# Seven pairs of attention column blocks of the input projection, in part as seven products of 2x2 blocks

## The chip, the cores and the metric

The kernel runs on one core of one Trainium2 chip. The metric is the device time of one execution in microseconds. The median of three runs of the kernel before is 1010.01 us (1008.98 to 1010.36).

## The reference, cut to what matters

One layer of a hybrid decoder trunk, all in float32: 16 learned meta tokens stand ahead of 512 tokens (528 in all), and the width is 2048. After an RMS norm one input projection feeds three mixers side by side: gated DeltaNet (6 heads of 128), GLA linear attention (5 heads, 64 by 128) and forgetting attention (5 heads of 128). Each mixer's output is multiplied by the SiLU of its own gate columns; the three are joined, go through one output projection, and are added to the input; a final RMS norm follows.

```
proj = (rms_norm(x) @ w_in)                       # 528 x 2048 @ 2048 x 7585
(dq, dk, dv, dz, db, da, gq, gk, gv, gz, gl, fq, fk, fv, fz, ff) = split_cols(proj)
o_dn  = gated_delta_rule(silu(conv(dq, dk, dv)), ...)  -> head norm -> * silu(dz)
o_gla = gla(gq, gk, gv, gates of gl)                   -> head norm -> * silu(gz)
o_fox = softmax(fq.fk / sqrt(d) + c_t - c_s, causal) @ fv           -> * silu(fz)
out   = rms_norm(x + concat(o_dn, o_gla, o_fox) @ w_out)[:, 16:]
```

For the change, the columns `fk`, `fv`, `fq` and `fz` of the attention heads matter: each is a block of 128 columns per head, a 2048 x 128 matrix that multiplies the 528 (or, where meta tokens aren't needed, 512) columns of x transposed.

## The kernel before, in words

**Precision.** TensorE works on float32 values rounded to a shorter form (fp32r). So each operand is split exactly into a high and a low part, and each product is three matmuls: high by high, high by low, low by high. `split` makes the parts of a weight tile: a cast on ScalarE (L150) and a subtraction on VectorE (L151). x is kept on chip as 16 k-tiles of 128 rows in two parts, `xh[k]` and `xl[k]`, of 528 columns each.

**Input projection.** It goes block by block (128 columns). `inproj` loads the block's weights in two halves of 128 x 1024 (eight k-tiles, 512 KB, buffer `raw`), splits them (`whi`, `wlo`; two buffers of each kind, pool `wp`), and accumulates in PSUM tiles `pp` of the pool `psb` (four banks). A block that needs the meta tokens is two column ranges of 264, so 16 x 3 x 2 = 96 matmuls; one without them is a single range of 512, 48 matmuls (all at L207). `evac` (L325, L327) or `gate_z` multiplies the result by the row scale `rstd` on VectorE.

**Order.** The program is written group by group: DeltaNet heads 0 to 2 (keys, values, queries, a triangular inverse, then the recurrence over four blocks of tokens), DeltaNet heads 3 to 5, the GLA gates, three GLA pairs, and five attention heads (`fox_head`: keys, values, queries, gate; then per block of 128 queries scores, softmax and transposes, and at the end the sum over values). A scheduler orders every engine's instructions ahead of time by a simulated timeline; an engine then runs its queue strictly in that order. TensorE's order mixes one head's mixer with the projection of the blocks to come. `behind` and the tables `PLACE` and `PM` tie a few mixer matmuls behind a given number of projection matmuls. `paced` ties an instruction behind the last split so far.

**Output projection.** Eight of its sixteen input blocks (six DeltaNet, two GLA) are already computed as seven products of 2x2 blocks instead of eight. Sums of the weights for this are made by `weight_sums(j, half)` beside the attention: four loads of 256 KB, four subtractions on VectorE (L432), four stores to HBM tile `tw`. Before, heads 0 to 3 make two each (table `SUMS`). Sums of the left operands are made by `first_sums` (L459, L460) in head 4 on VectorE; the gated mixer outputs `zs` that they read stay on chip all the time, in the pool `zp` of eleven buffers. The matmuls of the output projection stand at L1068, the last VectorE and GpSimd steps at L1082 to L1092.

**Pools that the change touches:** `zp` (mixer gates), `six` (eight large buffers), `row` (seven buffers of one row of 531), `psb` (four PSUM banks of the projection).

Of the kernel before, what the change touches and what calls it, by code (L numbers as in the profile page):

```python
# [8 lines left out]
F32 = mybir.dt.float32  # L9
F32R = mybir.dt.float32r  # L10
# [21 lines left out]

DN_HEADS, GLA_HEADS, FOX_HEADS = 6, 5, 5
SH = 8
R0 = 32
R1 = R0 + 17

# [41 lines left out]
def tile_hybrid_trunk(ctx, tc, xT, xtok, mtok, w_gate, w_in, w_out, w_dn, consts, lmask, fin_w, out, dbg=None):  # L79
# [4 lines left out]
    cst = pool("cst", 1)  # L84
    hp = pool("hp", 2 * KT)
    wp = pool("wp", 2)
    zp = pool("zp", 11)
    six = pool("six", 8)
    wk = pool("wk", 2)
    psb = pool("psb", 4, space=PSUM)  # L90
# [3 lines left out]
    def row(name, dt=F32):  # L94
        return wk.tile([P, 3 + T], dt, tag="row", bufs=7, name=name)
# [246 lines left out]
    def gate_z(kind, h, t=None):  # L342
        parts = inproj((kind, h), meta=False)
        p_, t0, n = parts[0]
        z = row(f"z{kind}{h}")[:, :T]
        V.tensor_tensor(out=z[:, :S], in0=p_, in1=rstd[:, t0 : t0 + n], op=ALU.mult)
        if t is None:
            t = zp.tile([P, S], F32, tag="zs", name=f"zs{kind}{h}")
        silu(t, z[:, :S], f"{kind}{h}")
        zs[kind, h] = t  # L350

# [53 lines left out]
    dump("gcol", gcol[:, 0:4])  # L405


    def conv_silu(key, blk, dst, meta=True):
# [17 lines left out]
    def weight_sums(j, half):  # L426
# [16 lines left out]
        sub(x, x, z)  # L443
        put(3, x)

    heads = ([("dz", h) for h in range(DN_HEADS)] + [("gz", h) for h in range(GLA_HEADS)]
             + [("fz", h) for h in range(FOX_HEADS)])
    sub = lambda o, a, b: V.tensor_tensor(out=o, in0=a, in1=b, op=ALU.subtract)
    pairs = range(SH // 2)
    t0, t1 = slice(0, 256), slice(256, 512)  # L450
# [2 lines left out]
    def first_sums():  # L453

        s1 = six.tile([P, SH // 2, 256], F32, tag="six", name="s1")
        for j in pairs:
            a, b = (zs[heads[2 * j + i]] for i in range(2))
            raw[j] = r = dict(a11=a[:, t0], a12=b[:, t0], a21=a[:, t1], a22=b[:, t1], s1=s1[:, j], s3=a[:, t1])
            V.tensor_tensor(out=r["s1"], in0=r["a21"], in1=r["a22"], op=ALU.add)  # L459
# [283 lines left out]
    def gla_pair(p):  # L743
# [31 lines left out]
        a32 = wk.tile([P, 8, 32], F32, tag="a32", bufs=1, name=f"a32{p}")  # L775
        G.memset(a32, 0.0)
        at = ats[0]

# [114 lines left out]
        for e in range(ne):  # L893
# [11 lines left out]
                PE.transpose(pt[:, b * P : (b + 1) * P], on[:, b * P : (b + 1) * P], ident)  # L905
            o = zs["gz", 2 * p + e]
            V.scalar_tensor_tensor(out=o, in0=pt, scalar=glw[:, 0:1], in1=o, op0=ALU.mult, op1=ALU.mult)


    def fox_head(h):  # L910
        qk = six.tile([P, 3, T], F32, tag="six", name=f"fqk{h}")
        kT, qT = qk[:, 0], qk[:, 2]
        evac(inproj(("fk", h)), kT)

        v = row(f"vf{h}")[:, :T]
        evac(inproj(("fv", h)), v)
        pv = psm.tile([P, 512], F32, tag="m", name=f"pvf{h}")
        for b in range(NB):
            PE.transpose(pv[:, b * P : (b + 1) * P], v[:, bsl(b)], ident)
        vhi, vlo = (row(f"v{n}{h}", dt=F32R)[:, :S] for n in ("hi", "lo"))  # L920
        v3 = t15(f"v3{h}", (P, P))
        A.copy(vhi, pv)
        V.tensor_tensor(out=vlo, in0=pv, in1=vhi.bitcast(F32), op=ALU.subtract)
        A.copy(v3, pv[:, 3 * P :])
        v4 = t15(f"v4{h}", (P, 2 * NB, NM))
        G.tensor_copy(v4, v[:, 0:NM].unsqueeze(1).to_broadcast([P, 2 * NB, NM]))
        pw = psm.tile([P, 512], F32, tag="m", name=f"pwf{h}")
        PE.transpose(pw[:, :P], v4.rearrange("p b t -> p (b t)"), ident)
        vm = t15(f"fvm{h}", (P, 2, P), F32R)
        A.copy(vm[:, 0], pw[:, :P])  # L930
        V.tensor_tensor(out=vm[:, 1], in0=pw[:, :P], in1=vm[:, 0].bitcast(F32), op=ALU.subtract)
        evac(inproj(("fq", h), meta=False), qT, scale=float(P) ** -0.5)
        cc = six.tile([P, 2 * T + S], F32, tag="six", name=f"fc{h}")
        z = wk.tile([P, S], F32, tag="gd", name=f"fz{h}") if h < 2 else cc[:, T + S : T + 2 * S]
        gate_z("fz", h, z)
# [6 lines left out]
        if h == FS:  # L942
            first_sums()
        if h in SUMS:
            for j, half in SUMS[h]:
                weight_sums(j, half)
# [52 lines left out]
    PM = (308, 319)  # L999
    for g in range(2):  # L1000
# [15 lines left out]
    qts += [kq[0][:, 2 * S :], kq[1][:, :S]]  # L1016
    ats.append(kq[1][:, S:].rearrange("p (n t) -> p n t", t=P))
    for p in range(3):
        gla_pair(p)
    for h in range(GLA_HEADS):  # L1020
        dump(f"ogl{h}", zs["gz", h])
    for h in range(FOX_HEADS):
        fox_head(h)
    for h in range(FOX_HEADS):
        dump(f"ofx{h}", zs["fz", h])
# [4 lines left out]
            mybir.DependencyClass.NoSync, mybir.DependencyReason.DATA), reason="behind")  # L1030


    plain = heads[SH:]
    NP = len(plain)
    EARLY, LAST = NP - 2, NP - 6
# [17 lines left out]
    free = []  # L1053

    def begin(tb, cc, load=True):
        if len(acc) < 11 - SH:
            acc[tb, cc] = zp.tile([P, S], F32, tag="zs", name=f"acc{cc}{tb}")
# [173 lines left out]
def _layout(x, meta_tokens, norm_w, w_in, conv_w, a_log, dt_bias, dn_norm_w, w_gk2, b_gk,  # L1231
# [11 lines left out]
    wo = w_out[0][SH * P :].reshape((16 - SH) // 2, 2, P, 4, 512)  # L1243
# [44 lines left out]
```

## Time and profile before

| | |
|---|---|
| median of 3 runs | 1010.01 us |
| the profiled execution | 1010.53 us |
| its span, first to last instruction | 1008.8 us |
| TensorE matmul busy | 995.7 us, 7614 matmuls |
| VectorE, ScalarE, GpSimd busy | 618.2, 433.1, 138.6 us |
| bytes moved by DMA | 128.13 MB |

Busy time is the union of an engine's instructions. Matmuls overlap one another in it, so the mean duration of one is longer than the time that it adds; the distance between two starts is the better measure. In the groups, a row names the line, the engine, the operation, what it writes and reads, the shape and the count; then busy time and the mean of one in ns, and the idle time before them with what ended it. In timelines a row starts with its start and duration in us.

### The profile page before, as it was taken

How to read it: one execution, taken by the hardware profiler on the slowest of the kernel's cores; microseconds unless marked ns; L12 is line 12 of the kernel's file. 1: busy time of each engine (PE TensorE's matmuls, PEld its weight loads, DVE VectorE, ACT ScalarE, POOL GpSimd, SP SyncE). 2: the span in 40 equal slices, each digit the busy share in tenths (PEclk: the TensorE clock that was granted, in tenths of full speed). 3: DMA queues.
4: the chain of work that ended last, by engine and by line, in shares of the span. 5: the costliest groups of instructions: out<-in, count | busy, mean ns of one | idle time of the engine just before them, and what ended most of it. 6: DMA issues, size and time to landing. Idle time of an engine off the chain costs nothing.

```text
span 1008.8 us, 19003 instructions
## 1 busy us (share of the span) xinstructions
PE 995.7 (99%) x7614; PEld 898.7 (89%) x7614; DVE 618.2 (61%) x1342; ACT 433.1 (43%) x948; POOL 138.6 (14%) x141
## 2 busy tenths in 40 slices
PE   9999999999999999999999999999999999999996
PEld 7899999899999888898989988889898988888885
DVE  6366767865566985244646474655363747677673
ACT  7654533434456334244445444342323244354354
POOL 0021411211112322101111010100101010000060
PEclk9999999999999999999999999999999999999999
DMA  9623233233222223231221272543362635466634
GB/s 351 229 67 119 82 93 96 102 101 104 75 86 75 94 90 101 68 94 59 84 64 50 66 244 82 189 138 93 120 226 95 237 119 188 127 193 226 181 109 167
DMA packets 53357, 128.13 MB, mean 127 GB/s; under 512 B 11949, under 2 KB 15197, under 8 KB 53268
## 3 DMA queue, kind: packets, MB, share of 16 engines
q1 hardware_dynamic: 39008, 115.30, 34.5%
q10 hardware_dynamic: 14260, 11.61, 4.1%
q8 instruction: 60, 0.98, 0.4%
q14 instruction: 29, 0.24, 0.1%
HBM read 113.32 MB, written 13.44 MB: 126 GB/s over the span
## 4 chain that ended last, share of the span: by engine, by line
PE 92%; DVE 3%; ACT 1%; DMA 1%; POOL 1%; issue 1%; ACTq 1%; SPq 0%; DVEq 0%; POOLq 0%
PE pp L207 57%; PE pa L1068 5%; PE pq L1068 4%; PE pp L261 4%; PE pt L1068 4%; PE ps L1068 2%; PE pss L822 1%; PE pr L1068 1%; POOL stgz L334 1%; PE pgate L361 1%; PE pfo L990 1%; PE pfa L957 1%; DVE wlo L151 1%; DVE ot L556 1%; PE pg L523 1%
## 5 line engine op out<-in xcount | busy, mean ns | idle before, releaser
L207 PE MATMUL pp<-xl,whi 128*128 128x264 f32 (+2 forms) x1456 | 378.1, 310 | 0.0
L207 PE MATMUL pp<-xh,whi 128*128 128x264 f32 (+2 forms) x1456 | 376.3, 310 | 0.8 <-DVE fqk L325 0.7
L207 PE MATMUL pp<-xh,wlo 128*128 128x264 f32 (+2 forms) x1456 | 375.4, 309 | 0.4 <-DVE wlo L151 0.4
L207 PEld LDWEIGHTS pp<-xh,whi 128*128 128x128 f32 x1456 | 243.1, 188 | 15.1 <-issue 1.4
L207 PEld LDWEIGHTS pp<-xl,whi 128*128 128x128 f32 x1456 | 244.3, 189 | 13.6 <-issue 0.2
L207 PEld LDWEIGHTS pp<-xh,wlo 128*128 128x128 f32 x1456 | 243.7, 188 | 14.1 <-DVE wlo L151 0.8
L150 ACT CAST whi<-raw 128x1024 fp32r<-128x1024 f32 x110 | 115.3, 1048 | 184.7 <-PE pp L207 158.1
L151 DVE TENSOR_TENSOR wlo<-raw,whi 128x1024 fp32r<-128x1024 f32 x110 | 134.4, 1222 | 88.8 <-ACT whi L150 78.2
L334 POOL TENSOR_SCALAR stc<-cv 128x528 f32<-128x528 f32 (+1 forms) x18 | 28.2, 1566 | 138.2 <-DVE cv L418 115.2
L418 DVE SCALAR_TENSOR_TENSOR cv<-pb,cpk,cv 128x528 f32<-128x528 f32 (+1 forms) x54 | 40.7, 755 | 0.7
L1068 PE MATMUL pa<-whio,ol 128*128 128x512 f32 x72 | 28.5, 396 | 0.0
L1068 PE MATMUL pa<-wloo,oh 128*128 128x512 f32 x72 | 28.3, 393 | 0.0
L325 DVE TENSOR_TENSOR pb<-pp,rstd 128x264 f32<-128x264 f32 (+1 forms) x36 | 13.7, 423 | 23.3 <-PE pp L207 23.3
L432 DVE TENSOR_TENSOR ws<-ws 128x512 f32<-128x512 f32 x32 | 21.6, 686 | 9.7 <-DMA ws<-in_w_dn 9.6
L150 ACT CAST whis<-raws 128x1024 fp32r<-128x1024 f32 x16 | 16.8, 1051 | 24.8 <-PE pq L1068 9.7
L151 DVE TENSOR_TENSOR wlos<-raws,whis 128x1024 fp32r<-128x1024 f32 x16 | 19.5, 1222 | 12.7 <-ACT whis L150 12.7
L1068 PE MATMUL pa<-whio,oh 128*128 128x512 f32 x72 | 26.6, 399 | 0.0
L977 ACT CAST fphi<-pfx 128x384 fp32r<-128x384 f32 (+2 forms) x20 | 8.0, 399 | 41.0 <-PE pfx L974 38.2
L966 ACT ACTIVATE fp<-fp,fsm 128x144 f32<-128x144 f32 (+3 forms) x20 | 11.5, 574 | 29.8 <-DVE fsm L965 29.7
L150 ACT CAST whio<-rawo 128x1024 fp32r<-128x1024 f32 x13 | 13.7, 1051 | 24.1 <-PE pa L1068 12.8
L334 POOL TENSOR_SCALAR stfz<-zfz 128x512 f32<-128x512 f32 x5 | 10.6, 2126 | 94.9 <-ACT whi L150 47.8
L1092 POOL TENSOR_TENSOR acc<-acc,fw 128x512 f32<-128x512 f32 x3 | 4.6, 1564 | 135.2 <-ACT sqf L1089 135.2
(439 smaller groups left out, 1642.7 us busy)
## 6 DMA issues: line engine op xcount, KB each, us to landing
raw<-in_w_in SPq DMA_DIRECT2D x110, 512.0 KB, 3.3
ws<-in_w_dn SPq DMA_DIRECT2D x32, 256.0 KB, 4.7
tw<-ws SPq DMA_DIRECT2D x32, 256.0 KB, 3.5
rawo<-in_w_out SPq DMA_DIRECT2D x13, 512.0 KB, 3.4
raws<-tw SPq DMA_DIRECT2D x12, 512.0 KB, 4.6
xt<-in_xtok SPq DMA_DIRECT2D x8, 512.0 KB, 8.7
rawa<-in_w_dn SPq DMA_DIRECT2D x8, 512.0 KB, 3.6
xs<-in_xT SPq DMA_DIRECT2D x7, 528.0 KB, 7.1
```

Of the source, the lines that this page charges most:

```text
L150: pace[0] = A.copy(hi, raw).ins
L151: pace[1] = V.tensor_tensor(out=lo, in0=raw, in1=hi.bitcast(F32), op=ALU.subtract).ins
L207: mm = PE.matmul(p_[:, :nt], wt[:, j * m : (j + 1) * m], xx[k][:, t0 : t0 + nt], start=(k == 0 and wt is hi and xx is xh), stop=(k == KT - ...
L261: mm = PE.matmul(ps[:, :S], wt[:, j * P : (j + 1) * P], xx[k][:, NM:T], start=(k == 0 and wt is hi and xx is xh), stop=(k == KT - 1 and wt ...
L325: V.tensor_tensor(out=o, in0=p_[rows], in1=rstd[rows, t0 : t0 + n], op=ALU.mult)
L334: G.tensor_scalar_max(t, src, LOW)
L361: PE.matmul(pgate[a][:, :HT], wg[k // 8][:, k % 8, :], xx[k][:, a * HT : (a + 1) * HT], start=(k == 0 and xx is xh), stop=(k == KT - 1 and ...
L418: V.scalar_tensor_tensor(out=c, in0=pb[:, t0 + w : w + T], scalar=cwc[:, blk, w : w + 1], in1=c, op0=ALU.mult, op1=ALU.add)
L432: sub = lambda o, a, b: V.tensor_tensor(out=o, in0=a, in1=b, op=ALU.subtract)
L523: PE.matmul(pg[:r, j * r : (j + 1) * r], kT[:, j, ts], kT[:, j, ts], start=True, stop=True)
L966: A.activation(pr[:, : m + P], pr[:, : m + P], AF.Exp, bias=sm[:, 2:3], accum_out=sm[:, 3:4])
L1068: PE.matmul(p_, o_[:, s], w_, start=(first and n == 0), stop=(last and n == 2), skip_group_check=True)
```

## The change

Seven pairs of attention blocks, (values, gate) of head 1 and (keys, queries) and (values, gate) of heads 2 to 4, are computed together by a new function, `inproj_pair`. For eight of the sixteen k-tiles (0 to 3 and 8 to 11) it uses a scheme of seven products of 2x2 blocks: the two halves of these k-tiles, the two blocks of columns, and the two halves of the tokens (264 each) make the 2x2 matrices. Weight sums for this (`in_sums`: four loads, four VectorE operations, four stores to the HBM tile `ti`, for each pair) are made during DeltaNet, one pair at a time by the table `AHEAD`. Sums of x (`x_sums`, on GpSimd with casts on ScalarE and subtractions on VectorE) are made during GLA and attention head 0; one more sum (`x_last`) overwrites the upper half of `xh`, `xl` of k-tiles 0 to 3 once the last plain block of head 1 has read them. The other eight k-tiles are plain products in the same PSUM banks. Results are combined on ScalarE and VectorE and then multiplied by `rstd` (on GpSimd, the queries on VectorE).

The eight gated outputs that the output projection needs in sums are stored to HBM (`zd`) and loaded again ahead of it; `zp` has twelve buffers of 528 columns; `first_sums` moves to the third step of the output projection and to GpSimd; the attention heads' large buffer is taken one head ahead; the output weight sums are made in heads 1 to 3 alone, some of them ahead of the head. The scratch tile `a32` of GLA shares the buffer `ot`.

```
+    PAIRS = [(h, *b) for h in range(H1, FOX_HEADS) for b in (("fk", "fq"), ("fv", "fz"))][SKIP:]   # H1 = SKIP = LATE = 1, NK = 4, KC = 512
+    def in_sums(n):
+        h, one, two = PAIRS[n]
+        x, y, z = stage(f"is{n}")                       # three buffers of zp
+        get = lambda o, key, half: nc.sync.dma_start(out=o, in_=w_in[BLOCK_OF[key, h], half][:, :KC])
+        put = lambda i, t: nc.sync.dma_start(out=ti[n][:, i], in_=t)
+        two_ = lambda o, a, b, op: paced(V.tensor_tensor(out=o, in0=a, in1=b, op=op))
+        get(x, two, 0); get(y, two, 1); get(z, one, 0)
+        two_(y, x, y, ALU.add); two_(x, z, x, ALU.subtract); put(0, y)
+        two_(z, y, z, ALU.subtract); put(2, x); put(1, z)
+        get(x, one, 1); two_(x, x, z, ALU.subtract); put(3, x)
...
+    def inproj_pair(n, c1, c2, tmp):
...
+        def tile_of(name, *parts):                      # raw, hi, lo of wp; one split for each 512 columns
...
+        def mm(p_, w, xx, first=False, last=False, cols=slice(0, HT)):   # 4 k-tiles x 3 matmuls
...
+        w1, w2 = tile_of("1", both(b1, head_))
+        mm(a, w1, xs_(up, lo_), True, True)
+        A.copy(ta, a[:, :HT])
+        mm(b, w2, xs_(dn, lo_), True)
+        def two():
+            d = bank("d")
+            w1, w2 = tile_of("2", ti[n][:, 0:2])
+            mm(d, w1, sums("t1"), True, True)
+            A.copy(tb, d[:, :HT])
+            mm(a, w2, sums("t2"), False, True)
+            V.tensor_tensor(out=tb, in0=a[:, :HT], in1=tb, op=ALU.add)
+        def three():
+            c = bank("c")
+            w1, w2 = tile_of("3", both(b1, rest_))
+            mm(b, w1, xs_(r0, lo_)); mm(b, w2, xs_(r1, lo_), False, True)
+            V.tensor_tensor(out=c1[:, lo_], in0=b[:, :HT], in1=ta, op=ALU.add)
+            mm(c, w1, xs_(r0, hi_), True); mm(c, w2, xs_(r1, hi_))
+        for f in (three, two) if n < LATE else (two, three):
+            f()
+        w1, w2 = tile_of("4", ti[n][:, 2:4])
+        mm(a, w1, xs_(up, hi_), False, True)
+        A.copy(ta, a[:, :HT])
+        mm(c, w2, xs_(dn, hi_), False, True)
+        V.tensor_tensor(out=c1[:, hi_], in0=c[:, :HT], in1=tb, op=ALU.add)
+        w1, w2 = tile_of("5", w_in[b2, 0][:, rest_], w_in[b2, 1][:, head_])
+        mm(d, w1, xs_(r0, hi_)); mm(a, w2, sums("t4"), cols=dead); mm(a, w1, xs_(r0, lo_), cols=dead)   # dead: 248 columns
+        w1, = tile_of("6", w_in[b2, 1][:, rest_])
+        mm(d, w1, xs_(r1, hi_), False, True)
+        V.tensor_tensor(out=c2[:, hi_], in0=d[:, :HT], in1=ta, op=ALU.add)
+        mm(a, w1, xs_(r1, lo_), False, True, cols=dead)
+        A.copy(c2[:, dead], a[:, dead])
...
-            V.tensor_tensor(out=r["s1"], in0=r["a21"], in1=r["a22"], op=ALU.add)
-            sub(r["s3"], r["a11"], r["a21"])
+            G.tensor_tensor(out=r["s1"], in0=r["a21"], in1=r["a22"], op=ALU.add)
+            G.tensor_tensor(out=r["s3"], in0=r["a11"], in1=r["a21"], op=ALU.subtract)
...
-    SUMS = {h: [(h, 0), (h, 1)] for h in range(4)}
-    FS = 4
+    SUMS = {1:[(0,1)],2:[(1,1),(3,0)],3:[(2,1),(3,1)]}
+    AHEAD = {(0,0):(0,),(0,1):(1,),(0,2):(2,),(1,0):(3,),(1,1):(4,),(1,2):(5,),(1,3):(6,),("f",1):((0,0),),("f",2):((1,0),),("f",3):((2,0),)}
+    XSUM = {1: (0,), 2: (1,2), 9:(3,)}
...
         st = dn_keys(g)
+        ahead(g, 0)
         dn_values(g, st)
+        ahead(g, 1)
         dn_queries(g, st)
+        ahead(g, 2)
         dn_inverse(g, st)
+        ahead(g, 3)
         dn_mix(g, st)
+        for h in range(H * g, H * g + H):
+            nc.sync.dma_start(out=zd[h], in_=zs["dz", h])
...
+    for i in range(SH):                                  # ahead of the output projection
+        zs[key] = zp.tile([P, T], F32, tag="zs", name=f"zr{i}")[:, :S]
+        nc.sync.dma_start(out=zs[key], in_=zd[i])
...
-    steps.append(lambda: rest(EARLY, EARLY + 1))
+    steps.append(lambda: (first_sums(), rest(EARLY, EARLY + 1)))
```

More of the change, by code (lines that the diff above doesn't have):

```diff
@@ new lines, in tile_hybrid_trunk, with x_last @@
+    xr = {}
+    def x_last(last):
+        f = lambda u: u[:, HT:].bitcast(F32)
+        for k in range(NK):
+            if not last:
+                if k % 2 == 0:
+                    t = row(f"xe{k}")
+                xr[k] = a = t[:, HT * (k % 2) : HT * (k % 2) + HT]
+                V.tensor_tensor(out=a, in0=f(xh[k + 8]), in1=f(xh[k]), op=ALU.subtract)
+                V.tensor_tensor(out=a, in0=a, in1=f(xl[k + 8]), op=ALU.add)
+                V.tensor_tensor(out=a, in0=a, in1=f(xl[k]), op=ALU.subtract)
+            else:
+                A.copy(xh[k][:, HT:], xr[k])
+                V.tensor_tensor(out=xl[k][:, HT:], in0=xr[k], in1=f(xh[k]), op=ALU.subtract)
@@ L907, in gla_pair @@
             V.scalar_tensor_tensor(out=o, in0=pt, scalar=glw[:, 0:1], in1=o, op0=ALU.mult, op1=ALU.mult)
+            if 2 * p + e < SH - DN_HEADS:
+                nc.sync.dma_start(out=zd[DN_HEADS + 2 * p + e], in_=o)
+    ahead_ = {}
     def fox_head(h):
-        qk = six.tile([P, 3, T], F32, tag="six", name=f"fqk{h}")
+        if h not in ahead_:
+            ahead_[h] = six.tile([P, 3, T], F32, tag="six", name=f"fqk{h}")
+        qk = ahead_.pop(h)
         kT, qT = qk[:, 0], qk[:, 2]
-        evac(inproj(("fk", h)), kT)
@@ L915, in fox_head @@
[L915 to L932, printed above, removed]
+        def values(v):
+            pv = psm.tile([P, 512], F32, tag="m", name=f"pvf{h}")
+            for b in range(NB):
+                PE.transpose(pv[:, b * P : (b + 1) * P], v[:, bsl(b)], ident)
+            vhi, vlo = (row(f"v{n}{h}", dt=F32R)[:, :S] for n in ("hi", "lo"))
+            v3 = t15(f"v3{h}", (P, P))
+            A.copy(vhi, pv)
+            V.tensor_tensor(out=vlo, in0=pv, in1=vhi.bitcast(F32), op=ALU.subtract)
+            A.copy(v3, pv[:, 3 * P :])
+            v4 = t15(f"v4{h}", (P, 2 * NB, NM))
+            G.tensor_copy(v4, v[:, 0:NM].unsqueeze(1).to_broadcast([P, 2 * NB, NM]))
+            pw = psm.tile([P, 512], F32, tag="m", name=f"pwf{h}")
+            PE.transpose(pw[:, :P], v4.rearrange("p b t -> p (b t)"), ident)
+            vm = t15(f"fvm{h}", (P, 2, P), F32R)
+            A.copy(vm[:, 0], pw[:, :P])
+            V.tensor_tensor(out=vm[:, 1], in0=pw[:, :P], in1=vm[:, 0].bitcast(F32), op=ALU.subtract)
+            return vhi, vlo, v3, vm
@@ L1022, in tile_hybrid_trunk @@
     for h in range(FOX_HEADS):
+        ahead("f", h)
+        x_sums(XSUM.get(3 + h, ()))
+        if h == H1 and XLAST:
+            x_last(False)
         fox_head(h)
```

149 lines of the change are left out of this document (140 added, 9 removed).

## The prediction

> **What bounds the kernel now.** I read the page first (parts 1, 2 and 4), for which engine carries the end.
>
> ```profile
> span 1008.8 us, 19003 instructions
> ...
> PE 995.7 (99%) x7614; PEld 898.7 (89%) x7614; DVE 618.2 (61%) x1342; ACT 433.1 (43%) x948; POOL 138.6 (14%) x141
> ...
> PEclk9999999999999999999999999999999999999999
> ...
> PE 92%; DVE 3%; ACT 1%; DMA 1%; POOL 1%; issue 1%; ACTq 1%; SPq 0%; DVEq 0%; POOLq 0%
> ```
>
> TensorE is busy 99% of the span at full granted clock, and 92% of the chain that ended last is its own work. Time goes only where matmuls go, or where TensorE is made to wait. Next the groups by line with shapes kept apart:
>
> ```profile
> L207 PE MATMUL pp<-xl,whi 128*128 128x264 f32 x960 | 218.3, 288 | 0.0
> L207 PE MATMUL pp<-xh,whi 128*128 128x512 f32 x304 | 120.8, 397 | 0.7 <-DVE fqk L325 0.7
> ```
>
> L207 is the input projection. Each form stands three times (high weights by both parts of x, low weights by the high part). The means (288 and 397 ns) are latencies of overlapping matmuls and no price. The price is the distance between starts, from TensorE's timeline in attention:
>
> ```profile
> 692.53 0.41 PE L207 MATMUL pp<-xl,whi 128*128 128x264 f32 x2
> ...
> 696.42 0.40 PE L207 MATMUL pp<-xh,wlo 128*128 128x264 f32 x2
> ...
> 700.19 0.39 PE L207 MATMUL pp<-xl,whi 128*128 128x512 f32 x1
> ...
> 708.07 0.39 PE L207 MATMUL pp<-xh,wlo 128*128 128x512 f32 x1
> ...
> 715.15 0.28 PE L990 MATMUL pfo<-fphi,vhi 128*128 128x256 f32 x1
> ...
> 715.50 0.39 PE L991 MATMUL pfo<-fp,v 128*128 128x128 f32 x2
> ```
>
> From 692.53 to 696.42 lie 16 rows of two: 3.89 us / 32 = 121.6 ns for 264 columns. From 700.19 to 708.07 lie 34 matmuls: 231.8 ns for 512. Three of 256 columns take 0.35 us, 117 ns each. So a matmul costs (231.8 - 121.6) / 248 = 0.444 ns a column and some 4 ns beside; cutting one in two is nearly free. A 248-column one would be 121.6 - 16 x 0.444 = 114.5 ns; its upper bound is the 121.6 of the nearest width, should the weight load that each matmul has set the pace.
>
> **TensorE's work in the change.** A pair before is one block over all 528 tokens (16 k-tiles x 3 x 2 = 96 matmuls of 264) and one over 512 (16 x 3 = 48 of 512): 96 x 121.6 + 48 x 231.8 = 22.80 us. The new function issues 15 groups of 4 k-tiles x 3 = 12: 7 products over eight of the sixteen k-tiles where four products twice over would be 8, and 8 plain groups for the rest. Twelve groups have 264 columns, three 248: 144 x 121.6 + 36 x 114.5 = 21.63 us. That is 1.17 us less a pair, **8.2 us** in seven; at 121.6 ns for all it is 0.91 a pair, 6.4 us.
>
> The Trainium skill, "TensorE: Matmul & The Clock Gate", section "Wait — 56ns, not 53.3ns?", puts the distance of warm matmuls at columns / 2.4 GHz and about 2.5 ns; the rows are 8 to 16 ns longer, and by it the saving would be an estimated 8.0 us.
>
> **Weights in smaller portions.** The forty-two weight tiles of the pairs are cast and subtracted in 512-column halves; prices:
>
> ```profile
> L150 ACT CAST whi<-raw x110: 1028/1049/1072, 47.6 to 816.7; 128x1024 fp32r<-128x1024 f32 x110
> ...
> L150 ACT CAST wlh<-rawl x6: 617/618/621, 959.3 to 971.3; 128x512 fp32r<-128x512 f32 x6
> ```
> ```profile
> L151 DVE TENSOR_TENSOR wlo<-raw,whi x110: 1198/1224/1475, 48.6 to 817.8; 128x1024 fp32r<-128x1024 f32 x110
> ...
> L151 DVE TENSOR_TENSOR wll<-rawl,wlh x6: 684/692/1198, 959.9 to 973.4; 128x512 fp32r<-128x512 f32 x6
> ```
>
> A pair has 11 halves: 11 x 0.62 = 6.8 us of ScalarE (before 4 x 1.05 = 4.2) and 11 x 0.69 = 7.6 us of VectorE (before 4.9). What matters is the rhythm. Before, a tile feeds TensorE for 48 x 121.6 = 5.8 us; now four of the six in a pair feed 24 matmuls, 2.9 us. How a tile is supplied, in the timelines:
>
> ```profile
> 736.24 1.05 ACT L150 CAST whi<-raw 128x1024 fp32r<-128x1024 f32 x1 [2.03 <-PE pp L207]
> ```
> ```profile
> 737.83 1.21 DVE L151 TENSOR_TENSOR wlo<-raw,whi 128x1024 fp32r<-128x1024 f32 x1
> ```
> ```profile
> 743.07 0.41 PE L207 MATMUL pp<-xh,whi 128*128 128x264 f32 x2
> ```
>
> The cast starts when TensorE releases a buffer, the low part is ready 2.8 us later (739.04), and the first matmul of that tile comes at 743.07: 4.0 us to spare. With a short tile the first half's cast is ready after 0.62 us and needed after 2.9: 2.3 us to spare; its low part, ready after 1.3, is read 8 matmuls later, at 3.9: 2.6 to spare. In the row above the subtraction came 0.54 us after the cast's end; delays of that size are covered. A raw tile's load is issued after the split two tiles earlier and has two tile times, 5.8 us in the worst place:
>
> ```profile
> raw<-in_w_in SPq DMA_DIRECT2D x110, 512.0 KB, 3.3
> ws<-in_w_dn SPq DMA_DIRECT2D x32, 256.0 KB, 4.7
> tw<-ws SPq DMA_DIRECT2D x32, 256.0 KB, 3.5
> ```
>
> From the release, split 2.0 and load 3.3 end at 5.3 us; 4.7 would end at 6.7, 0.9 past the release that it should meet, within the 2.3. The queues fill up:
>
> ```profile
> 325.00:375.00 50.00, 50.00 (x250) 41.24 (x247) 44.52 (x119) 18.96 (x39) 15.72 (x15) 1.00 0.26 82
> 668.00:828.00 160.00, 160.00 (x1025) 144.81 (x1025) 81.92 (x198) 53.71 (x106) 12.17 (x12) 1.00 0.42 142
> ...
> 400.00:640.00 240.00, 236.99 (x2687) 218.43 (x2687) 124.78 (x277) 102.02 (x283) 26.63 (x21) 1.00 0.28 90
> ```
>
> ```profile
> 728.13 0.16 DVE L967 RECIPROCAL fsm<-fsm 128x1 f32<-128x1 f32 x1 [1.63 <-ACT fp L966]
> ```
> ```profile
> L1049 ACT CAST a<-zsdz x9: 389/400/402, 840.6 to 916.0; 128x256 fp32r<-128x256 f32 x9
> ```
>
> Columns are PE, PEld, DVE, ACT, POOL busy. Attention heads 1 to 4 lie in 668 to 828: VectorE 82 of 160 us. Added: 19 for the halves, about 3 for results and 5.5 for the eight subtractions that head 0 had; 110 of some 152, 72%. ScalarE: 54 + 18 + 28 copies of 0.40 = 83, 55%. Both still have room; an in-order queue at 72% will now and then hold a split for more than 2.3 us (behind the softmax's reciprocal, say, which sat 1.63 us waiting for its exponential). I take 0.5 us at a tenth of the 28 short tiles, **+1.4 us**; bounds 0 and 1 us at each, 28.
>
> PSUM: a pair takes all four banks of its pool, but the second is free after the third tile and the third after the fourth, so the next pair's first two banks wait for nothing; the 0.4 us copies between have 24 matmuls, 2.9 us, of cover, and if it were gone, 0.4 us a copy.
>
> **Sums and moved steps.**
>
> ```profile
> L432 DVE TENSOR_TENSOR ws<-ws 128x512 f32<-128x512 f32 x32 | 21.6, 686 | 9.7 <-DMA ws<-in_w_dn 9.6
> L325 DVE TENSOR_TENSOR pb<-pp,rstd 128x264 f32<-128x264 f32 x24 | 9.2, 425 | 16.9 <-PE pp L207 16.9
> ...
> L1092 POOL TENSOR_TENSOR accs<-accs,fw x9: 1281/1291/2349, 972.3 to 984.3; 128x512 f32<-128x512 f32 x9
> ```
>
> Weights: 7 x 4 operations of 0.686 = 19.2 us on VectorE, each set four loads and four stores on SP, all in DeltaNet. Before, stores waited little for VectorE (next row), and raw loads queue behind them. Queued behind the new operations on VectorE are the convolution and the inverse's recurrence, for whose end the triangular matmuls wait. VectorE is at 44.5 of 50 us in 325 to 375, but the sets are tied behind the last split of keys, values and queries, so most of them fall earlier. x sums: 28 adds on GpSimd of about 0.67 us (half of 1.29) and 12 casts and 12 subtractions in GLA and head 0, then 12 + 4 subtractions of 0.43; the last overwrite of x is needed only by the first pair's fourth tile, 96 matmuls (11.7 us) later. In GLA TensorE's own slack is thin:
>
> ```profile
> SPq L431 <- DVE ws L432: 11.0, 16, 2.1
> ```
> ```profile
> PE pss L822 <- issue: 1.5, 2, 1.3
> ...
> PE psn L694 <- ACT y L690: 0.6, 1, 0.6
> ```
>
> 400 to 640 has 3.0 us of TensorE idle, where the chain through scores and state is met just in time. The additions cannot add to TensorE's wait more than they queue ahead of it: 3 sets x 2.7 us = 8 us as upper bound; a changed order may also win back some of the 3.0 us. I take **+1.5 us**, bounds -2 and +8, near the low end because DeltaNet's window above shows TensorE busy 50.00 of 50 us even where VectorE is fullest.
>
> The eight gate rows go to HBM and return (16 DMAs of 256 KB on SP); their half-sums, which move from VectorE (next row) to GpSimd, are asked for after the third run of the output projection: 3 x 24 x 231.8 ns = 16.7 us of cover against 3.3 to 4.7 for a load. Nothing, then; if the loads stood behind others on SP until that cover is gone, the last one's 4.7 us.
>
> ```profile
> L459 DVE TENSOR_TENSOR s<-zsdz,zsdz x3: 418/419/419, 834.4 to 835.0; 128x256 f32<-128x256 f32 x3
> ```
>
> **Sum:** -8.2 + 1.4 + 1.5 = -5.3. The profiled execution is 1010.53 (span 1008.8 and 1.7 around it), so 1005.2 there; it lies 0.5 over the median 1010.01, so **1004.7 us**.
>
> **Rivals.** *Supply becomes the bound (slower).* At 2.9 us a tile, cast, subtraction, raw load and release no longer close the loop beside softmax and sums. For it: 72% on VectorE, loads of 4.7 us, four of six tiles short. Against: 2.3 us to spare. At 0.5 us on each of 28 short tiles it costs 14: 1004.7 - 1.4 + 14 = **1017**; it decides from 0.29 us a short tile, where 8.2 is used up. *The sums disturb DeltaNet or GLA.* The 8 us bound taken in full: 1004.7 - 1.5 + 8 = **1011**, no change. For it: 44.5 of 50 us; against: the ties and idle VectorE before. *GpSimd holds up the splits (slower).* Eleven multiplications by the row scale, 1.3 us or more each, now run on GpSimd between splits; if each kept one split waiting past its slack, 11 x 1.3 = 14 us: **1017**. Against: the subtraction ran 1198 to 1475 ns over the kernel, 0.25 at most above its median, while GpSimd's adds went from 1291 to 2349; here GpSimd pays. The Trainium skill, "SBUF — State Buffer", section "Who interferes with whom", says that VectorE with two SBUF inputs and GpSimd reading SBUF exclude each other and the second to issue is blocked whole; the trace shows that for GpSimd alone. *That fewer columns are not run* can't be: the counts are in the code.
>
> **Chances and range.** Forecast 0.68; disturbed DeltaNet and GLA 0.12; supply 0.16; GpSimd 0.04. A change under 0.2%, 2 us, is about what a measurement of this kernel can't tell from none. So faster 0.68, same 0.12, slower 0.20. Low end: 8.2 saved and 1 won back, 1001; high end 1014, into the supply case, leaving out 0.15 above and 0.05 below.
>
> **What would show it.** Matmuls of the pairs 120 to 122 ns apart at 264 columns and near 114 at 248; some 21.6 us of them a pair; TensorE idle before its short tiles, released by the cast or the subtraction, under 2 us in all; none at DeltaNet's inverse. Wrong it is if TensorE's idle grows by over 6 us, or if the narrow matmuls stand further apart than 122 ns.

## The result, and the profile after

The changed kernel takes 1021.14 us (median of 6 runs, 1017.24 to 1021.99) beside 1009.31 for the kernel before (6 runs, 1008.19 to 1010.36): ratio 1.0111, 95% interval 1.0094 to 1.0129. It is slower by about 11.8 us, where 5.3 us less were forecast, and lies outside the forecast range of 1001 to 1014. The profiled execution took 1020.76 us.

The page of the changed kernel, the lines that answer to those of before:

```profile
span 1019.0 us, 19951 instructions
...
PE 992.3 (97%) x7866; PEld 907.2 (89%) x7866; DVE 674.8 (66%) x1449; ACT 460.9 (45%) x1041; POOL 195.2 (19%) x192
...
PEclk9999999999999999999999999999999999999999
...
PE 79%; DMA 8%; DVE 7%; ACT 2%; issue 1%; POOL 1%; SPq 1%; ACTq 0%; DVEq 0%; POOLq 0%
```

TensorE's time outside its instructions (span less busy) grows from 13.1 to 26.7 us, by more than the 6 us that the prediction named as a sign of being wrong, and its own share of the chain that ended last falls from 92% to 79%: DMA and VectorE now stand on it with 15%. TensorE is still the busiest engine by far; it is made to wait.

TensorE's timeline of a pair in head 2 gives the spacing of the new matmuls:

```profile
699.16 1.08 PE L516 MATMUL pp_a<-t,whi 128*128 128x248 f32 x8
700.09 0.62 PE L516 MATMUL pp_a<-t,wlo 128*128 128x248 f32 x4
700.54 0.28 PE L516 MATMUL pp_a<-xh,whi 128*128 128x248 f32 x1
...
709.79 1.14 PE L516 MATMUL pp_d<-t,whi 128*128 128x264 f32 x8
...
712.71 0.29 PE L516 MATMUL pp_b<-xh,whi 128*128 128x264 f32 x1
```

Twelve of 248 columns from 699.16 to 700.54 are 115 ns apart; 24 of 264 from 709.79 to 712.71 (the x8, x4, x8, x4 of two products) 121.7 ns. The matmuls cost what was forecast. The loss is in stretches around them; two windows show it, before (first row) and after (second), columns PE, PEld, DVE, ACT, POOL busy, clock, DMA share and GB/s:

```profile
640.00:830.00 190.00, 189.31 (x1168) 168.99 (x1167) 102.60 (x250) 63.40 (x123) 13.95 (x15) 1.00 0.47 157
```
```profile
640.00:830.00 190.00, 179.36 (x1399) 173.02 (x1399) 131.96 (x330) 84.45 (x200) 32.88 (x33) 1.00 0.63 207
...
400.00:425.00 25.00, 22.82 (x273) 19.44 (x274) 6.87 (x14) 7.33 (x12) 2.98 (x3) 0.93 0.23 72
```

From 640 to 830 us, the attention, TensorE is busy 10 us less, although VectorE is busy only 69% and ScalarE 44%. The waits of TensorE after, in 640 to 830 (line waited for: us in all, times, longest):

```profile
PE pp_a L516 <- DVE fqk L541: 1.9, 2, 1.6
PE pp_b L516 <- ACT whi L155: 1.8, 1, 1.8
PE pp_a L516 <- ACT fqk L558: 1.5, 1, 1.5
PE pp_b L516 <- DVE wlo L156: 1.1, 1, 1.1
PE pp_d L516 <- DVE wlo L156: 1.0, 1, 1.0
PE pp_d L516 <- ACT whi L155: 1.0, 2, 0.6
PE pfx L1177 <- DVE fmt L1172: 0.8, 2, 0.6
PE pfo L1194 <- ACT fp L1183: 0.8, 1, 0.8
PE pp_a L516 <- DVE fsm L1168: 0.7, 1, 0.7
```

They are many small ones, 10.6 us in all, on evacuations of PSUM banks (L541, L558), on casts and on low parts. Views around two of them follow: SyncE's queue, ScalarE, one piece of the chain that ended last, and VectorE.

```profile
744.68 3.83 SPq L594 DMA_DIRECT2D tw<-ws  x4
748.60 0.38 SPq L593 DMA_DIRECT2D ws<-in_w_dn  x1
749.08 1.29 SPq L504 DMA_DIRECT2D raw<-in_w_in  x2
750.66 3.40 SPq L594 DMA_DIRECT2D tw<-ws  x3
...
756.42 3.51 SPq L593 DMA_DIRECT2D ws<-in_w_dn  x4
759.98 0.43 SPq L504 DMA_DIRECT2D raw<-in_w_in  x1
```
```profile
766.53 1.14 ACT L155 CAST whi<-raw 128x512 fp32r<-128x512 f32 x2 [4.71 <-DMA raw<-in_w_in]
```
```profile
759.98 6.45 DMA raw<-in_w_in
```
```profile
743.96 0.69 DVE L595 TENSOR_TENSOR ws<-ws 128x512 f32<-128x512 f32 x1 [3.06 <-DMA ws<-in_w_dn]
...
745.87 0.43 DVE L541 TENSOR_TENSOR fqk<-pp_a,fqk 128x264 f32<-128x264 f32 x1
...
756.40 1.29 DVE L156 TENSOR_TENSOR wlo<-raw,whi 128x512 fp32r<-128x512 f32 x2 [1.08 <-ACT whi L155]
```

SyncE's queue runs in the order that the scheduler gave it. Loads of the weight tiles (L504) stand behind the stores of an output weight sum (L594) and its loads (L593), and an issue that waits holds up everything after it. The tile load issued at 759.98 had its buffer free since the subtraction that ends at 757.7: it stood 2.3 us behind four loads of sums, the second of which waited for a store to land. Then it took 6.45 us to land, at 766.43, where the median before is 3.3. ScalarE sat 4.71 us for it and TensorE 1.8. By these numbers the cast would have been in time without the 2.3 us in the queue, and also with a landing in 3.3 us; it was late by both together. On VectorE the subtraction at 743.96 waited 3.06 us for its own load, with the pair's evacuation L541 behind it; TensorE waited 1.6 us. SyncE's waits from 640 to 830:

```profile
SPq L504 <- DVE wlo L156: 40.0, 25, 4.3
SPq L594 <- DVE ws L595: 20.8, 15, 3.4
SPq L593 <- DMA tw<-ws: 11.1, 6, 2.2
```

The other stretch is the second inverse of DeltaNet, TensorE's wait and three of VectorE's rows before it:

```profile
PE pm L739 <- DVE iv L733: 3.0, 1, 3.0
```
```profile
314.02 1.29 DVE L429 TENSOR_TENSOR is<-is,is 128x512 f32<-128x512 f32 x2
...
323.84 0.69 DVE L429 TENSOR_TENSOR is<-is,is 128x512 f32<-128x512 f32 x1 [2.85 <-DMA is<-in_w_in]
326.68 0.69 DVE L429 TENSOR_TENSOR is<-is,is 128x512 f32<-128x512 f32 x1 [2.15 <-DMA is<-in_w_in]
```

The last two pair sums run at 314 to 327 us, ahead of the `an` products, and VectorE stands 5.0 us of that for their loads; the recurrence ends at 392.2 instead of 386.2 us and the first triangular matmul, at its fixed place 319 in TensorE's order, waits 3.0 us. The 25 us behind show a granted clock of 0.93.

### The profile page after: what moved, and what is told of

The parts are those of the page before. It is cut to its first block, busy times and chain, and to the rows that moved or that the text cites. A ratio compares the mean times of both kernels' runs of the same rounds, so it can differ in the third digit from the quotient of the medians.

```text
span 1019.0 us, 19951 instructions
## 1 busy us (share of the span) xinstructions
PE 992.3 (97%) x7866; PEld 907.2 (89%) x7866; DVE 674.8 (66%) x1449; ACT 460.9 (45%) x1041; POOL 195.2 (19%) x192
## 4 chain that ended last, share of the span: by engine, by line
PE 79%; DMA 8%; DVE 7%; ACT 2%; issue 1%; POOL 1%; SPq 1%; ACTq 0%; DVEq 0%; POOLq 0%
PE pp L212 39%; PE pa L1294 5%; PE pp L266 4%; PE pq L1294 4%; PE pt L1294 4%; PE pp_a L516 3%; DMA ws<-in_w_dn 3%; PE ps L1294 2%; DVE wlo L156 2%; PE pp_c L516 2%; PE pp_b L516 2%; PE pp_d L516 1%; DMA raw<-in_w_in 1%; POOL stgz L339 1%; PE pss L987 1%
## 5 line engine op out<-in xcount | busy, mean ns | idle before, releaser
L212 PE MATMUL pp<-xl,whi 128*128 128x264 f32 (+2 forms) x1120 | 285.1, 307 | 0.0
L212 PE MATMUL pp<-xh,whi 128*128 128x264 f32 (+2 forms) x1120 | 283.4, 306 | 0.8 <-DVE fqk L330 0.8
L212 PE MATMUL pp<-xh,wlo 128*128 128x264 f32 (+2 forms) x1120 | 282.9, 306 | 0.6 <-DVE wlo L156 0.6
L155 ACT CAST whi<-raw 128x1024 fp32r<-128x1024 f32 (+1 forms) x159 | 130.1, 840 | 179.3 <-PE pp L212 112.9
L156 DVE TENSOR_TENSOR wlo<-raw,whi 128x1024 fp32r<-128x1024 f32 (+1 forms) x159 | 153.9, 982 | 81.9 <-ACT whi L155 75.7
L212 PEld LDWEIGHTS pp<-xh,whi 128*128 128x128 f32 x1120 | 186.9, 189 | 10.6 <-DVE fqk L330 1.0
L212 PEld LDWEIGHTS pp<-xh,wlo 128*128 128x128 f32 x1120 | 187.0, 189 | 9.8 <-DVE wlo L156 1.0
L212 PEld LDWEIGHTS pp<-xl,whi 128*128 128x128 f32 x1120 | 187.4, 189 | 8.9 <-issue 0.2
L516 PE MATMUL pp_a<-xh,whi 128*128 128x264 f32 (+1 forms) x112 | 28.6, 287 | 2.6 <-DVE fqk L541 1.9
L516 PE MATMUL pp_a<-xl,whi 128*128 128x264 f32 (+1 forms) x112 | 28.0, 281 | 0.0
L156 DVE TENSOR_TENSOR wlos<-raws,whis 128x1024 fp32r<-128x1024 f32 x16 | 19.3, 1222 | 10.8 <-ACT whis L155 10.6
```

What stands on the lines that cost most here:

```text
L155: pace[0] = A.copy(hi, raw).ins
L156: pace[1] = V.tensor_tensor(out=lo, in0=raw, in1=hi.bitcast(F32), op=ALU.subtract).ins
L212: mm = PE.matmul(p_[:, :nt], wt[:, j * m : (j + 1) * m], xx[k][:, t0 : t0 + nt], start=(k == 0 and wt is hi and xx is xh), stop=(k == KT - ...
L516: m = PE.matmul(p_[:, cols], wt[:, j * P : (j + 1) * P], xx[j][part_][:, cols], start=first and i == 0, stop=last and i == len(todo) - 1, ...
```

## The experiments

Each kernel was timed beside the kernel before on the same chip. "Over before" is the difference of the two medians; the changed kernel is at +11.8.

**Which sums cost, or the short tiles themselves.** Theory A: the output weight sums' transfers and operations, queued among the short tiles. Theory C: the pair sums, which make the second inverse late. Rival B: the short tiles cannot be supplied, whatever runs beside them.

```
e1: SUMS = {}; no ("f", n) in AHEAD; products read w_dn as it is
e2: no pair numbers in AHEAD; tiles 2 and 4 read w_in as it is
e3: both
```

> Left out: the weight sums of the output projection beside the attention (their products read plain weight blocks of the same size instead, so the output is another). Theory A, that the loads and VectorE operations of these sums, queued between the short tiles, make TensorE wait in attention: most of the 12 us of waits that the changed kernel shows from 645 to 815 us go, about 1010 us (1008 to 1012). Theory B, that short tiles of 24 matmuls can't be supplied in time whatever stands beside them: the waits stay, 1017 to 1021.

> Left out: the weight sums of the pairs in DeltaNet (tiles 2 and 4 of a pair read plain weights of the same size, so the output is another). Theory C, that the last two sets of these sums push the second inverse of DeltaNet back behind the place that the fixed order gives it on TensorE (wait of 3.2 us at 399 us and a lower granted clock after it): that wait goes, 1014.5 to 1017 us. If it was the changed order alone: 1020 or more.

> Left out: both kinds of weight sums (the output is another). Theories A and C together: both waits go and what is left is TensorE's saving of 8.2 us with a few us of waits, 1002 to 1006 us. Theory B: over 1011 us, the waits of the pairs still there.

Without output sums 1010.75 (+0.3, ratio 1.0004, 0.9991 to 1.0017); without pair sums 1014.2 (+3.8, 1.0041, 1.0024 to 1.0058); without both 1005.35 (-5.1, 0.9942, 0.9922 to 0.9962). So output sums cost 11.5 us, pair sums 8.0, both together 16.9: they share some 2.6. All three lie at or within 0.3 us of what theories A and C expected. Waits and window of the kernel without both, attention:

```profile
PE pp_b L516 <- DVE wlo L156: 1.1, 1, 1.1
PE pp_a L516 <- ACT fqk L558: 1.0, 1, 1.0
```
```profile
640.00:830.00 190.00, 187.85 (x1480) 183.18 (x1480) 120.64 (x307) 90.02 (x210) 35.40 (x36) 1.00 0.43 135
```

Two waits, 2.1 us for 28 short tiles: B falls. The 512 KB tile loads take 3.9 us to land here in the median, against 3.3 in the kernel before. In e2 the wait at the inverse is gone and the attention's stay.

**Transfers or operations of the output sums.**

```
e5: sub(y, x, y); sub(x, z, x); sub(z, z, y); sub(x, x, z) left out
e6: the same four kept, on a buffer cleared by GpSimd; get() and put() left out; products read w_dn as it is
```

> Left out: the four VectorE subtractions of each output weight sum beside the attention; loads and stores stay, so the sums are wrong. Theory A1, that the loads and stores themselves (bursts of 256 KB transfers between the pairs' weight loads, in one SP queue) starve the short tiles: stays at 1017 to 1021 us. Theory A2, that the subtractions are the cost, since they stand in VectorE's queue waiting for their loads with the pairs' splits and sums behind them: falls to 1010 to 1014 us.

> The other half: the subtractions stay (on a cleared buffer), the loads and stores of the output weight sums are left out, and the products read plain weights. A1: 1009 to 1012 us, like leaving the sums out. A2 in the form that VectorE's time itself is short: 1016 to 1020. A2 in the form that VectorE waits for loads: 1009 to 1012 too, and then the loads-only run tells.

Transfers alone: 1015.69 (+5.9, 1.0061, 1.0041 to 1.0080), 5.5 above e1 and between the two expectations. TensorE's longest wait there, 3.1 us, is for a tile load that took 7.3 us to land; the slowest in the attention before took 4.2. Operations alone: 1012.04 (+2.2, 1.0014, 1.0005 to 1.0024), 1.9 above it, with VectorE busier than in the changed kernel (140.6 of 190 us). Together they cost 11.5, more than 5.5 + 1.9. That the rest comes of stores that wait for operations, and operations that wait for loads, is what the rows above suggest.

**The inverse.**

```
e4: pair sums 5 and 6 in AHEAD ("g",0), ("g",1), at GLA
e7: PM = (308, 345)
```

> The last two sets of pair sums (5 and 6) move from behind the queries and the inverse of the second DeltaNet group to the first two GLA pairs; the computation is whole. Theory C: the inverse ends as early as before the change, no wait of 3 us at it, 1014 to 1017 us. If the sums only change place with their cost, because GLA is as tight: 1019 to 1022.

> The changed kernel whole, with one number changed: the second inverse's first matmul is tied behind 345 projection matmuls instead of 319. Theory C, that TensorE's fixed order meets the inverse about 3 us before it is ready: the wait at 399 us and the lower clock after it go, 1016 to 1018 us. If the late inverse costs its time in the recurrence anyway: 1019 to 1022.

e4: 1019.51 (+9.1, 1.0085, 1.0055 to 1.0115), as the rival expected. The recurrence is on time again (386.7), but the transfers of its result took until 398.3 beside those of the sums, and TensorE still waits 2.0 us. e7: 1018.21 (+8.4, 1.0078, 1.0061 to 1.0095), just above the 1016 to 1018 expected; the recurrence is as late as in the change, but the wait shrinks to 0.3 us and the clock stays up:

```profile
400.00:425.00 25.00, 24.69 (x301) 21.38 (x299) 7.30 (x15) 7.44 (x12) 3.25 (x4) 1.00 0.26 73
```

**The sums somewhere else.**

```
e8:  six output sums and pair sums 5, 6 in GLA, in buffers of zp that wait for the second inverse; two output sums in head 0
e13: e9 (below) with four output sums in head 0, two in head 1, one each in heads 2 and 3
```

> The computation whole; six of the eight output weight sums and sets 5 and 6 of the pair sums are made in GLA, in zp buffers that are free there and only after the second inverse; the other two output sums in head 0; no sums beside the pairs. Theories A and C together: the waits at the inverse and in the pairs go, GLA pays 1 to 4 us, 1005 to 1009 us. If the sums cost the same wherever they stand: 1016 or more.

> Nothing is left out. As the kernel whose output sums' transfers are issued by GpSimd, place 345 (1012.6, kernel before 1010.05), but four of the eight output sums are formed in attention head 0 and two in head 1, where the weight tiles are long or half of them are, and two in heads 2 and 3. Theory (the sums cost where tiles are short): the wait of 2.7 us at 762 and some of the 1 us waits go: 1008 to 1010. Rival (what is left has nothing to do with the place of the sums, as the first pairs' own waits of 1.3 and 1.7 us and the GLA stage): 1012 to 1013. Against: six buffers of the shared pool are used earlier, in head 0, which can hold up its own steps: 1014.

Both miss: 1035.84 (1.0253, 1.0223 to 1.0282) and 1018.26 (1.0083, 1.0057 to 1.0108). In e8 TensorE waits all along (3.6 us for evacuations of blocks in GLA, 2.6 for zz, 3.1 for casts of pairs); in e13 the waits moved to head 1, 655 to 678. A place with long tiles is not free if the chain there is met just in time.

**Which queue: issue and subtraction apart.** All three have place 345, so e7 is their base.

```
e9:  get, put = nc.gpsimd.dma_start(...)    (sums' transfers leave SyncE)
e10: sub = G.tensor_tensor(...)             (subtractions leave VectorE)
e11: both
```

> Nothing is left out. Against the kernel in which only the place of the second inverse was moved to 345 (1018.2, kernel before 1009.8), one thing differs: the four loads and four stores of each output weight sum are issued from GpSimd's queue instead of SyncE's. Theory SP (the stores, and the fourth load that must wait for a store, stand in SyncE's queue and hold up the loads of the weight tiles behind them): the cast's wait for its raw tile (2 us in one place) goes, and with it most of what the loads cost alone (4.9 us): 1012 to 1014. Theory V (VectorE stands with a subtraction at its head that waits 3 us for its load, and the evacuations of the pairs behind it): unchanged, 1017 to 1019, and the 3 us waits of the subtractions remain. Rival traffic (the bytes themselves on the rings): unchanged too.

> Nothing is left out. Against the kernel in which only the place of the second inverse was moved to 345 (1018.2), one thing differs: the four subtractions of each output weight sum are GpSimd's instead of VectorE's; the transfers stay with SyncE. Theory V: the waits of TensorE for evacuations that stood behind a subtraction (1.75, 1.2, 1.7 us and smaller ones) go: 1010 to 1013. Theory SP: a subtraction on GpSimd is slower than 0.7 us, so stores and the fourth load wait longer in SyncE's queue: 1017 to 1021, with more waits of casts for raw tiles. Rival GpSimd (the multiplications of the pairs by rstd and the masks queue behind subtractions that wait): new waits of TensorE for these, 1018 or more.

> Nothing is left out. Both of the two last: subtractions by GpSimd and transfers from GpSimd's queue, place 345. If the queues of VectorE and SyncE are the whole cost of the output weight sums, what is left is the kernel without any sums (1005.35) with what the pair sums cost (about 3 us with the later place): 1007 to 1010, that is level with the kernel before or faster. If the traffic of the loads and stores is a cost by itself: 1012 to 1016. If GpSimd becomes the bound: 1018 or more, with TensorE's waits on GpSimd's results.

e9: 1012.57 (+2.5, 1.0025, 1.0010 to 1.0040), some 5.6 us below e7 for the same bytes, as the theory of SyncE's queue expected. TensorE's waits for casts of tiles fall from 1.2 to 0.2 us, although the tile loads take much the same to land (medians of the three kinds 4.3, 5.1 and 3.5 us in e7, 4.0, 4.3 and 4.1 in e9). But the issuer is not all that changed. The scheduler gave VectorE another order, too. In e7 the first subtraction of a sum is VectorE's next instruction behind an evacuation at 735.81 and waits 3.71 us for its load, with L541 behind it; in e9 the same subtraction comes several steps behind that evacuation (734.15), at 736.46, just ahead of L541, and waits for nothing. VectorE's waits for the sums' loads fall from 17.7 to 6.4 us, and TensorE's for L541, 3.2 us in e7, are gone. The page of e9 also puts these transfers on another kind of queue (software_dynamic, 5120 packets where there were 9216).

e10: 1025.27 (1.0154, 1.0119 to 1.0189); e11: 1028.76 (1.0183, 1.0160 to 1.0205). Rows of e10, the group of the subtractions and TensorE's worst waits:

```profile
L595 POOL TENSOR_TENSOR ws<-ws 128x512 f32<-128x512 f32 x32 | 46.3, 1454 | 53.0 <-DMA ws<-in_w_dn 44.9
```
```profile
PE pfx L1177 <- DVE fmt L1172: 6.1, 3, 3.1
PE pp_b L516 <- ACT whi L155: 5.7, 1, 5.7
```

A subtraction takes 1.45 us on GpSimd where VectorE took 0.75, and stores wait longer for it (54.8 us in 28 against 21.4 in 14 in e7). So e9 shows that the issuer matters, and not by which way: SyncE's queue, VectorE's new order and the other kind of queue changed together. With the operations on GpSimd the kernel was slower than e9 whoever issued the transfers (e10, e11), which leaves open what VectorE's waits for the sums' loads cost.

**Fewer pairs.**

```
e12: H1 = 2; pair sums 5 and 6 not formed (five pairs); PM = (308, 345)
e14: the same with the transfers of e9, but PM = (308, 319)
```

> Nothing is left out. The change with five pairs instead of seven: attention head 1 is projected block by block as before, and pair sums 5 and 6, which ran during the second inverse, are not formed. Place of the inverse as in the change (319). TensorE saves 5 x 1.17 = 5.9 us. Theory A+C (the output sums beside short tiles, and the pair sums beside the inverse): the inverse is on time, so its 5 us go; of the eight output sums half now run beside the long tiles of head 1: 1008 to 1011. Rival B (each pair costs more than it saves, whatever runs beside it): five sevenths of the change's loss, 1009.8 + 8 = 1018.

> Nothing is left out. Five pairs (1014.9 with SyncE issuing, kernel before 1010.05), with the output sums' transfers issued by GpSimd. Its waits were 3.36 us for a raw tile, 2.1 for an evacuation, 1.2 for a buffer of the scores, all between 712 and 760. Theory SP: the first goes, and most of the others: 1009 to 1011. If the traffic of the sums or the short tiles are the cost by themselves: 1014 to 1015.

The recorded expectation of e12 gives place 319; the kernel that ran had 345. e12: 1014.87 (+4.8, 1.0046, 1.0031 to 1.0062), between the two expectations: the inverse is on time, but a cast waits for its raw tile (TensorE 3.2 us at 758) and an evacuation behind a subtraction (1.9). e14: 1011.49 (+1.3, 1.0014, 1.0000 to 1.0027), 3.4 less. The cast's wait is gone, and the inverse is on time in both, but two things differ, issuer and place, so the 3.4 us are not the issuer's alone for certain.

**VectorE's order.**

```
e16: e9, subtractions emitted one and two steps after their loads
e17: the same on e14
e18: e16, each subtraction also ordered behind a later VectorE instruction
e19: the same on e17
```

> Nothing is left out. Seven pairs, place 345, transfers issued by GpSimd (1012.6), and the subtractions of each output sum are emitted later: the loads as before, three subtractions one step later (a block of the attention or a pair's end), the fourth another step later, so that VectorE does not reach a subtraction before its load has landed. Theory V (what is left is VectorE standing with a subtraction at its head): the 2.7 us at 762 go, and the subtractions no longer wait 1.7 to 3 us: 1007 to 1010. Rival (VectorE's time itself, or the short tiles): 1012 to 1014.

> Nothing is left out. Both of the two last with five pairs: GpSimd issues, subtractions emitted later, place of the inverse as in the change. No pair sums run beside the second inverse. If both queues and the inverse are the whole loss, TensorE's saving of 5.9 us is left less about 2 us of first waits: 1005 to 1008, faster than the kernel before. If the short tiles cost by themselves: 1010 to 1013.

> Nothing is left out. Seven pairs, place 345, transfers issued by GpSimd (1012.6), and the subtractions of each output sum ordered on VectorE behind a later instruction: the first three behind the subtraction of the first attention block after the loads' issue or the last evacuation of a pair, the fourth behind the next one. Theory V (VectorE standing with a subtraction that waits for its load): VectorE's waits for these loads (6.4 us in six) go, the 2.7 us of TensorE at 762 too: 1009 to 1011. Rival (VectorE's time, the short tiles): 1012 to 1013, with as much idle TensorE.

> Nothing is left out. The same order with five pairs and the place of the change (1011.5 without it). VectorE's waits for the loads of the sums were 14.5 us in seven there, and TensorE waited 1.8 and 2.1 us at 698 and 714, both behind such a subtraction. Theory V: both go: 1007 to 1009. Rival: 1011 to 1012.

e16 and e17 tell nothing: the order on VectorE came out as in e9 and e14, since the schedule doesn't follow the order of the text. They are repeats, 1012.75 against 1012.57 and 1012.09 against 1011.49. e18 and e19 do change the order: 1012.11 (1.0022, 1.0011 to 1.0034) and 1011.34 (1.0014, 1.0002 to 1.0026). In e18's profiled execution VectorE's waits for the loads fall from six to two (6.4 to 3.9 us) and the 2.6 us wait on fmt to 0.4:

```profile
DVE ws L595 <- DMA ws<-in_w_dn: 3.9, 2, 3.7
```
```profile
PE pp_d L516 <- ACT whi L155: 1.2, 2, 0.8
PE pp_b L516 <- DVE wlo L156: 1.1, 1, 1.1
PE pp_a L516 <- ACT fqk L558: 1.0, 1, 1.0
PE pfx L1199 <- DVE fmt L1194: 0.4, 1, 0.4
```

But that execution, 1009.34 us, is the fastest of its seven (1009.34 to 1015.08), and the medians do not separate. So VectorE's head of queue is seen in the traces as a wait and not shown as a cost of its own in the times. No version with its sums intact is faster than the kernel before; the nearest, e14, e17 and e19, are slower by 0.1%, and the intervals of e14 and e17 reach 1.0000.

## Why the prediction was wrong, point by point

**TensorE's work in the change: right.** 121.7 and 115 ns were measured for 121.6 and 114.5; the 8.2 us are saved. They appear net only without the sums: -5.1 in e3, which is -8.2 with 2.1 us of named waits and 1.0 that has no name, within the interval of that run.

**Weights in smaller portions: the size was wrong.** Forecast +1.4 for 28 tiles. The tiles by themselves cost 2.1 (e3), so the slack of 2.3 us held for nearly all of them. With the output sums beside them the waits come to some 11 us. The failed step is "From the release, split 2.0 and load 3.3 end at 5.3 us", and it failed twice. The issue was taken as immediate; the load at 759.98 stood 2.3 us in SyncE's queue after its buffer was free. And the 3.3 us did not hold: the pairs' loads of 512 KB have a median of 3.9 us without any sums (e3) and of 4.2 (from `w_in`) and 4.8 (from `ti`) in the change, and this one took 6.45, more than the 4.7 that the prediction allowed for. The prediction quoted the row of SyncE's waits for the subtractions (11.0 us, 16 times, longest 2.1) and called it little. With tiles of 5.8 us it was little; a longest of 2.1 is most of a slack of 2.3 us. After, in the attention alone, it is 20.8 us with a longest of 3.4, and 11.1 more for the load that waits for a store. e9 wins 5.6 us, with the reservation above. VectorE's share was right (69% for 72) and ScalarE's lower (44% for 55); an engine's share says nothing about the head of its queue.

**PSUM at nothing: wrong.** The prediction gave the copies "24 matmuls, 2.9 us, of cover, and if it were gone, 0.4 us a copy". The evacuations stood behind other work on VectorE, and TensorE waited 1.9 us for L541 and 1.5 for the copy L558. L541 stood behind a subtraction of a sum. L558 waited for L549, which stood behind steps of the softmax; 1.0 us of that wait is there without any sums, too (e3). An evacuation costs its place in the queue, not its duration.

**Sums and moved steps: wrong place, too low.** "Tied behind the last split of keys, values and queries, so most of them fall earlier" does not hold for sets 5 and 6, which ran at 314 to 327 ahead of the inverse. Forecast +1.5 with bounds -2 and +8; all seven sets cost 8.0 by e2, the upper bound. Of that 3.4 is the wait at the fixed place with the lower clock behind it (e7), and up to 2.6 is what the two kinds of sums share; for the rest no run names the cause. The prediction counted the additions' own time and not their waits for loads. It had no term for a drop of the clock, and none for this: that a step written to follow at a fixed place in TensorE's order turns 6 us of lateness into a wait.

**Reload of gate rows and the half-sums on GpSimd at nothing:** no wait of TensorE points to them.

**Rivals.** "Supply becomes the bound" (1017, 0.16) had the sign and nearly the size, and its point of decision, 0.29 us a short tile, was passed. But not as told: the loop of cast, subtraction, load and release does close (e3); it is held up by what the sums add, tile loads issued late and landing late among it. "Sums disturb DeltaNet or GLA" (1011, 0.12) was true as well, and both came at once; the forecast treated them as alternatives. "GpSimd holds up the splits" did not show: none of TensorE's waits in the change is for GpSimd's multiplications.

**What stays open.** Between e9 (+2.5) and e3 (-5.1) lie 7.6 us. e9's attention shows 4.6 us less TensorE work than e3's in 640 to 830, and e18's fastest execution 1.6 less; the ten executions of e9 spread over 6.6 us (1008.52 to 1015.09), the four of e3 over 3.2. That transfers which land a little later now hit tiles that are met just in time is argued from this, not shown. Pair sums left out with the issuer of e9 was not tried, nor the issuer of e9 with VectorE's order of e7 held, which would part queue and order.

## What to carry to other kernels

When a change halves the time that a tile feeds the busiest engine, work out again the slack of every in-order queue on the tile's way, the issuing queue first: a store that waits for its producer delays each load behind it, and a row of such waits that costs nothing today can cost much after the change. A load's time to land needs a margin as well: the same 512 KB took 3.3 us before and up to 4.8 in the median after. Each piece of moved work has to be held against its engine's order at the place where it lands, above all where another step has a fixed place. Two rivals that can happen together belong in the sum together. And when an experiment changes one word of the program, compare the order on the engines before and after: the scheduler may have changed more.

## What the runs showed of the hardware

After a wait of 3.0 us TensorE's clock fell to a mean of 0.93 over 25 us; after one of 0.3 us (e7) it stayed at 1.00. At the same place it fell to 0.93 after 3.2 us (e5) and to 0.86 after 2.9 (e1), and stayed at 1.00 after 2.7 (e6) and 2.0 (e4). In e10, after the wait of 5.7 us, 264-column matmuls stand 220 ns apart from 686.4 to 690.0 us and then 122 again. A loss of 0.07 of 25 us is 1.75 us, what 3.5 us at half speed would lose; the loss in e1 is twice that. The Trainium skill, "TensorE: Matmul & The Clock Gate", section "What's actually happening", has half speed after an idle window of some 3.4 us; the size of the loss agrees but for e1, while the waits of 2.9 to 3.2 us seen here are slightly shorter than the window.

Changing the issuer gained 5.6 us with the same bytes, although each issue on GpSimd took longer (a median of 0.54 us against 0.43):

```profile
L593 POOL DMA_DIRECT2D ws<-in_w_dn x32: 536/541/773, 646.6 to 805.3; - x32
```
```profile
L593 SPq DMA_DIRECT2D ws<-in_w_dn x32: 332/425/514, 656.2 to 811.0; - x32
```

The first row is e9's, the second the changed kernel's. The Trainium skill, "DMA: Bandwidth & Descriptors", section "Rules for kernel authors", says that another issuer saves only the sequencer's issue time; here the issue time rose and the time fell. That the waits that left SyncE's queue are the reason is argued above and not isolated.
